# Buffers kept across stages, and a second pool for modulation weights, in a two-block transformer kernel

## The chip, the cores and the metric

The kernel runs on one core of one Trainium2 chip. The metric is the device time of one execution in microseconds (us). The core has five engines that run their own instruction queues and meet at semaphores: TensorE (PE; its weight loads are shown apart as PEld), VectorE (DVE), ScalarE (ACT), GpSimd (POOL) and SyncE (SP). In this kernel SP issues nearly all DMA transfers, in the order of its queue.

## What is computed

The input is one sequence of 512 tokens, 1024 wide, in float32. The reference, cut to the calls that matter:

```python
def first_block(x, c, ...):
    mod = (jax.nn.silu(c) @ w_ada + b_ada)            # six vectors of 1024
    sh1, sc1, gt1, sh2, sc2, gt2 = jnp.split(mod, 6, axis=-1)
    h = rmsnorm(x, norm1_g) * (1.0 + sc1) + sh1
    z = h @ w_in
    ...
    mix = concat([rmsnorm(nsa_attention(...)), rmsnorm(s5_mixer(...))])
    x = x + gt1 * (mix @ w_o)
    h = rmsnorm(x, norm2_g) * (1.0 + sc2) + sh2
    a, v = jnp.split(causal_dwconv(h @ w_up, conv_w, conv_b), 2, axis=-1)
    x = x + gt2 * ((jax.nn.silu(a) * v) @ w_down)
    return rmsnorm(x, normf_g)

def second_block(x, ...):
    x = x + short_conv_mixer(rms_norm(x, conv_norm), ...)
    x = x + dilated_attention_mixer(rms_norm(x, attn_norm), ...)
    return x
```

nsa_attention has three branches (compressed keys, selected blocks, a window) with a gate each; s5_mixer is a linear recurrence over 32 groups of channels; the dilated attention has three groups of 16 heads.

## The kernel before

The program goes through four stages, one after the other: the mixer of the first block (attention and S5, about 0 to 375 us), its feed-forward part (to 751), the convolution mixer (to 1194) and the dilated attention (to 1822). All of x stays in SBUF as four tiles of 128 tokens.

**Gemms.** Every float32 factor is split into a high and a low part, and a product is three matmuls: high by high, high by low, low by high. `wload` (L100) brings a piece of weights, at most 128x1024 float32 (512 KB), into a "raw" buffer; ACT makes the high part `whi` from it, DVE the low part `wlo`. The raw buffers, three of them, belong to the weight pool `W["p"]`. The activations are kept transposed, eight planes of 128 channels by 512 tokens, also as a high and a low part: `xh` and `xl` for the normalized x, `hh` and `hl` for what the inner part of a stage makes.

**Normalizing at a stage's border.** `scaled` (L300) turns the sums of squares of two token tiles into scales, with a dozen small DVE operations, and multiplies x by them into two "adaw" buffers (L323). `norm_t` (L341) has PE transpose those (L350); ACT then writes xh and DVE xl (L358, or L364 where a shift is added). The first half of the tokens is normalized ahead, inside the last projection of the stage before (the list `ahead`); the second half (`second`) comes when the first gemms of the new stage have done the first half's tokens. In the mixer, `ahead` gets its entry (L1241) just before the last part of the output projection, `out_a(1)`. `residual` (L391) adds a projection's result to x and takes the sums of squares on ACT.

**Modulation.** The vectors shift, scale and gate come from w_ada, in twelve halves of four pieces of 512 KB. `ada_rows` (L214) loads a piece (L221) into an "adaw" buffer and multiplies it on PE (L223); `ada` (L248) adds up and spreads. There are two "adaw" buffers in the pool b1p, and three things share them: these pieces, the weights of the key and value compression (`hidden`, L962, with its load at L978 and matmuls at L981), and the normalized x (L323). The mixer's parts are written down in the order of two strings; the letters e, f, h, i, j, l, m and n stand for a modulation half each, a digit for a block of 128 queries of the attention, G for the S5 gate, w and x for parts of the output projection:

```python
ORDER = "kvDBCAKc1lbVda0g"
ORDER2 = "032jGn1mehfwxi"
```

**S5.** `core_b` (L919) works on eight channel groups at a time. It loads a matrix `mi` in eight strips (L932), multiplies on PE (L954, L957) and sends its result out and in again by DMA (`yd`, `yt`).

**Order and storage.** The framework's scheduler, which has its own estimate of each operation's time, sets the order of every engine's instructions once, when the program is built. On the chip each engine goes through its list in order and waits where something isn't ready. Pools open and close with their stage. A tile whose storage was used by an earlier tile waits for the earlier one's last reader: in a pool's own ring, that of the tile's last use; where a new pool lies over the storage of a closed one, those of the tiles that lay there. Before, xh, xl, hh and hl are made anew in each stage, in that stage's pool; the second attention also makes `kbh` and `kbl` there, blocked keys, which are zeroed by four MEMSETs on GpSimd (L1299), and loads a small tile of gains, `qkg` (L1293), which DVE scales (L1294).

## Time and profile before

| | us |
|---|---|
| median of three runs (1816.0, 1817.91, 1825.29) | 1817.91 |
| profiled execution | 1823.86 |
| its span | 1822.1 |
| PE busy | 1751.0 (96%) |
| DVE busy | 1095.5 (60%) |
| ACT busy | 845.7 (46%) |
| GpSimd busy | 184.3 (10%) |
| mean granted TensorE clock | 0.991 |

The span is the time from the first instruction of the profile to its last; the profiled execution's own time has 1.76 us around it. Busy times overlap, since the engines run side by side. An idle time in a row stands in brackets, with the operation that ended it; the granted clock is a share of full speed. In a timeline, consecutive instructions of one kind stand in one row, with their number behind an x.

### The profile page before, as it was taken

How to read it: one execution, taken by the hardware profiler on the slowest of the kernel's cores; microseconds unless marked ns; L12 is line 12 of the kernel's file. 1: busy time of each engine (PE TensorE's matmuls, PEld its weight loads, DVE VectorE, ACT ScalarE, POOL GpSimd, SP SyncE). 2: the span in 40 equal slices, each digit the busy share in tenths (PEclk: the TensorE clock that was granted, in tenths of full speed). 3: DMA queues.
4: the chain of work that ended last, by engine and by line, in shares of the span. 5: the costliest groups of instructions: out<-in, count | busy, mean ns of one | idle time of the engine just before them, and what ended most of it. 6: DMA issues, size and time to landing. Idle time of an engine off the chain costs nothing.

```text
span 1822.1 us, 25899 instructions
## 1 busy us (share of the span) xinstructions
PE 1751.0 (96%) x9588; PEld 1441.2 (79%) x9588; DVE 1095.5 (60%) x2720; ACT 845.7 (46%) x1679; POOL 184.3 (10%) x179
## 2 busy tenths in 40 slices
PE   5899989999999999899999999999999999999999
PEld 3787746888888888788888888878888888888877
DVE  8895766865545557643333333644766766666676
ACT  3532656564423445532322323445655655656653
POOL 3764202001100110000000000000000000000000
PEclk9998999999999999999999999999999999999999
DMA  8357750332333335333333323533222322322221
GB/s 341 95 152 199 230 176 12 102 122 92 94 92 104 95 102 173 106 104 95 102 93 99 98 93 104 152 107 102 85 78 82 94 73 80 91 74 91 82 65 64
DMA packets 86782, 200.21 MB, mean 110 GB/s; under 512 B 32000, under 2 KB 36864, under 8 KB 86656
## 3 DMA queue, kind: packets, MB, share of 16 engines
q1 hardware_dynamic: 86656, 198.57, 35.3%
q8 instruction: 75, 1.23, 0.3%
q14 instruction: 51, 0.42, 0.1%
HBM read 193.75 MB, written 4.78 MB: 109 GB/s over the span
## 4 chain that ended last, share of the span: by engine, by line
PE 85%; DVE 7%; DMA 4%; ACT 2%; issue 1%; POOL 1%; SPq 0%; DVEq 0%; ACTq 0%; POOLq 0%
PE bank L128 38%; PE bank L141 35%; DMA adaw<-in_w_ada_dram 2%; DVE wlo L95 1%; PE bank L1163 1%; PE bank L1500 1%; PE bank L1470 1%; PE bank L1580 1%; PE bank L223 1%; PE bank L1159 1%; PE bank L1558 1%; PE bank L1140 1%; PE bank L1569 1%; PE bank L1587 1%; ACT whi L59 1%
## 5 line engine op out<-in xcount | busy, mean ns | idle before, releaser
L95 DVE TENSOR_TENSOR wlo<-raw,whi 128x1024 fp32r<-128x1024 f32 (+1 forms) x287 | 350.1, 1220 | 302.5 <-ACT whi L59 288.5
L59 ACT ACTIVATE whi<-raw 128x1024 fp32r<-128x1024 f32 (+1 forms) x287 | 299.4, 1043 | 473.7 <-PE bank L128 265.2
L128 PE MATMUL bank<-xh,whi 128*128 128x512 f32 (+1 forms) x1120 | 291.2, 379 | 10.7 <-ACT xh L59 10.6
L128 PE MATMUL bank<-xl,whi 128*128 128x512 f32 (+1 forms) x1120 | 288.3, 375 | 7.0 <-DVE xl L364 6.8
L128 PE MATMUL bank<-xh,wlo 128*128 128x512 f32 (+1 forms) x1120 | 283.6, 374 | 0.0
L128 PEld LDWEIGHTS bank<-xh,whi 128*128 128x128 f32 x1120 | 204.3, 191 | 52.8 <-ACT xh L59 13.8
L128 PEld LDWEIGHTS bank<-xl,whi 128*128 128x128 f32 x1120 | 203.9, 189 | 47.1 <-DVE xl L364 8.8
L128 PEld LDWEIGHTS bank<-xh,wlo 128*128 128x128 f32 x1120 | 202.4, 189 | 37.7
L141 PE MATMUL bank<-whi,xh 128*128 128x512 f32 (+2 forms) x800 | 209.2, 361 | 2.5 <-ACT v L59 1.2
L141 PE MATMUL bank<-wlo,xh 128*128 128x512 f32 (+2 forms) x800 | 205.1, 356 | 0.0
L141 PE MATMUL bank<-whi,xl 128*128 128x512 f32 (+2 forms) x800 | 204.9, 355 | 0.0
L141 PEld LDWEIGHTS bank<-wlo,xh 128*128 128x128 f32 x800 | 135.5, 190 | 22.5 <-issue 1.6
L141 PEld LDWEIGHTS bank<-whi,xl 128*128 128x128 f32 x800 | 135.2, 190 | 22.5 <-issue 1.6
L141 PEld LDWEIGHTS bank<-whi,xh 128*128 128x128 f32 x800 | 128.8, 189 | 21.2 <-issue 3.9
L141 PE MATMUL bank<-wlo,hh 128*128 128x512 f32 x304 | 95.0, 389 | 0.0
L141 PE MATMUL bank<-whi,hl 128*128 128x512 f32 x304 | 94.9, 389 | 0.0
L198 DVE SCALAR_TENSOR_TENSOR cy<-bank,taps,cy 128x384 f32<-128x384 f32 (+3 forms) x176 | 72.9, 477 | 32.5 <-ACT cy L59 32.5
L59 ACT ACTIVATE P<-P,stat 128x128 f32<-128x128 f32 (+1 forms) x192 | 79.8, 419 | 21.9 <-DVE stat L1478 15.7
L141 PE MATMUL bank<-whi,hh 128*128 128x512 f32 x304 | 89.8, 389 | 0.0
L534 POOL TENSOR_TENSOR cy<-cy,sz 128x512 f32<-128x512 f32 x16 | 28.8, 1801 | 436.5 <-ACT sz L59 436.5
L141 PEld LDWEIGHTS bank<-whi,hl 128*128 128x128 f32 x304 | 57.1, 188 | 11.9
L141 PEld LDWEIGHTS bank<-wlo,hh 128*128 128x128 f32 x304 | 57.0, 188 | 11.8
(384 smaller groups left out, 2322.3 us busy)
## 6 DMA issues: line engine op xcount, KB each, us to landing
raw<-in_conv_w_in_dram SPq DMA_DIRECT2D x64, 512.0 KB, 3.7
raw<-in_w_pair_dram SPq DMA_DIRECT2D x64, 512.0 KB, 3.8
adaw<-in_w_ada_dram SPq DMA_DIRECT2D x48, 512.0 KB, 5.1
raw<-in_w_up_dram SPq DMA_DIRECT2D x44, 512.0 KB, 3.7
raw<-in_w_down_dram SPq DMA_DIRECT2D x30, 512.0 KB, 3.5
raw<-in_conv_w_out_dram SPq DMA_DIRECT2D x24, 512.0 KB, 3.7
raw<-in_w_o_dram SPq DMA_DIRECT2D x12, 512.0 KB, 4.2
x<-in_x_dram SPq DMA_DIRECT2D x8, 512.0 KB, 5.2
```

Source lines behind the costliest of these rows:

```text
L59: return nc.scalar.activation(o, i, fn, **kw)
L95: (eng or V).tensor_tensor(lo, src, f(hi), op=OP.subtract)
L128: mm(ps[:, tok], a[:, q, j * 128:(j + 1) * 128], b[:, k0 + q, tok], start=n == 0 and i == 0 and h != 1, stop=n == len(w) - 1 and i == 3 * ...
L141: mm(ps, a[:, base + k0 + q, tok], b[:, q, :], start=first and n == 0 and i == 0 and o == 0, stop=last and n == len(w) - 1 and i == 3 * kn ...
L198: V.scalar_tensor_tensor(o, i, t, o, op0=OP.mult, op1=OP.add)
L223: mm(pb[32 * q:32 * q + 32, :256], csil[:, r * 4 + q, 3 - i:35 - i], raw[:, q * 256:(q + 1) * 256], start=i == i0 and r == 0, stop=i > i0 ...
L534: P.tensor_tensor(y, y, sz, op=OP.mult)
L1140: mm(ps[:, :n], qs[:, h, qt], kk[:, br, kvh, 0:n], start=kk is ksh, stop=kk is ksl)
L1159: transpose(pt[:, s * 128:(s + 1) * 128], prs[hl][:, j * 128:(j + 1) * 128], ident)
L1163: mm(po[par * 64:par * 64 + 64, kvh * 256:(kvh + 1) * 256], vsw[:, j, br, kvh * 64:kvh * 64 + 64], ptt[:, par, :], start=False, stop=br == ...
L1470: mm(ps[:, :nk * 256], a[:, natural(i)], b[:, j0:i + 1].rearrange("p j h k -> p (j h k)"), start=n == 0, stop=n == 2)
L1500: mm(ps[:, r * 256:(r + 1) * 256], a[:, natural(2 * rr + r)], b[:, 2 * rr + r].rearrange("p h k -> p (h k)"), start=n == 0, stop=n == 2)
```

## The change

It has four parts.

1. ORDER2 has the last modulation half, `i`, ahead of the output projection's parts `w` and `x`.
2. `ada_rows` takes a second pool: of the two pieces of a row, the first goes to an "adaw" buffer as before, the second to a "raw" buffer of the weight pool.
3. Two pools, `hp` and `nx`, are opened ahead of the feed-forward stage and stay open to the end. `nx` holds nxh and nxl, the normalized x of the three later stages. `hp` holds h0 and h1, two tiles of 128x8x512: the first eight planes of hh and hl in the feed-forward stage (three more planes each are made in the stage's own pool), hh and hl in the convolution, and in the second attention yh and the blocked keys. Those are now one tile, zeroed by one MEMSET.
4. At the end of the mixer, the first half's scaling gets the scheduler's high priority.

```diff
-ORDER2 = "032jGn1mehfwxi"
+ORDER2 = "032jGn1mehfiwx"
...
-        def ada_rows(n0, n1, i0, pool, bufs, at):
+        def ada_rows(n0, n1, i0, pool, bufs, at, more=None):
...
-                    raw = pool.tile([128, 1024], F32, name="adaw", bufs=bufs)
+                    raw = more.tile([128, 1024], F32, name="raw") if more and r else \
+                        pool.tile([128, 1024], F32, name="adaw", bufs=bufs)
...
-            for pb in ada_rows(which * 4 + 2 * half, which * 4 + 2 * half + 1, 2 * half, b1p, 2, acc):
+            for pb in ada_rows(which * 4 + 2 * half, which * 4 + 2 * half + 1, 2 * half, b1p, 2, acc, W["p"]):
...
+        hp = top.enter_context(tc.tile_pool(name="hp", bufs=1, reuse_waits="tile"))
+        nx = top.enter_context(tc.tile_pool(name="nx", bufs=1, reuse_waits="tile"))
+
+        def hidden():
+            return [hp.tile([128, 8, S], F32R, name=n) for n in ("h0", "h1")]
+
+        def normed():
+            return [nx.tile([128, 8, S], F32R, name=n) for n in ("nxh", "nxl")]
...
-            xh = ffp.tile([128, 8, S], F32R, name="xh")
-            xl = ffp.tile([128, 8, S], F32R, name="xl")
-            hh = ffp.tile([128, 11, S], F32R, name="hh")
-            hl = ffp.tile([128, 11, S], F32R, name="hl")
+            xh, xl = normed()
+            hh, hl = (Planes([h[:, k] for k in range(8)] + [ffp.tile([128, S], F32R, name=f"{n}{k}") for k in range(3)])
+                      for n, h in zip(("hh", "hl"), hidden()))
...
-            xh = cvp.tile([128, 8, S], F32R, name="xh")
-            xl = cvp.tile([128, 8, S], F32R, name="xl")
-            hh = cvp.tile([128, 8, S], F32R, name="hh")
-            hl = cvp.tile([128, 8, S], F32R, name="hl")
+            xh, xl = normed()
+            hh, hl = hidden()
...
-        E["ahead"].append((E["scaled"](0), False))
+        with tc.high_priority():
+            E["ahead"].append((E["scaled"](0), False))
         out_a(1)
...
-        yh = pp.tile([128, 8, S], F32R, name="yh")
+        yh, kb = E["hidden"]()
         yl = Planes([None] * 8)
-        xh = pp.tile([128, 8, S], F32R, name="xh")
-        xl = pp.tile([128, 8, S], F32R, name="xl")
+        xh, xl = E["normed"]()
...
-        kbh = [pp.tile([128, 4, 2, 128], F32R, name=f"kbh{i}") for i in range(2)]
-        kbl = [pp.tile([128, 4, 2, 128], F32R, name=f"kbl{i}") for i in range(2)]
-        for t in kbh + kbl:
-            P.memset(f(t), 0.0)
+        P.memset(f(kb), 0.0)
+        kbs = [kb[:, 2 * i:2 * i + 2].rearrange("p a (b h k) -> p (a b) h k", b=2, h=2) for i in range(4)]
+        kbh, kbl = kbs[0:2], kbs[2:4]
```

The diff doesn't show the order that the scheduler makes of this. Three places follow, before and after. A row has the line of its own kernel (the changed one's lines are up to ten higher), the operation, what it writes and reads with buffer numbers, and the size; an x at the end counts equal rows.

First pair: SP's queue in the S5 stretch, around 140 us. `adaw` and `raw` from in_w_ada_dram are modulation pieces, in_w_c1_dram the compression weights of the values, in_w_in_g_dram and in_w_glu_dram ordinary weights. Before:

```order
L221 DMA adaw_1748<-in_w_ada_dram 128x1024
L221 DMA adaw_1754<-in_w_ada_dram 128x1024
L109 DMA raw_3233<-in_w_glu_dram 128x1024
L932 DMA mi_1888<-kd_118 16x8x128 x7
L978 DMA adaw_1829<-in_w_c1_dram 128x1024
L932 DMA mi_1888<-kd_118 16x8x128
L927 DMA uu_1942<-ud_116 128x512
L978 DMA adaw_1835<-in_w_c1_dram 128x1024
L960 DMA yd_117<-wk_1809 128x512
L978 DMA adaw_1841<-in_w_c1_dram 128x1024
L978 DMA adaw_1847<-in_w_c1_dram 128x1024
L932 DMA mi_1944<-kd_118 16x8x128 x8
```

After:

```order
L109 DMA raw_2151<-in_w_in_g_dram 128x840
L968 DMA yd_117<-wk_1570 128x512
L986 DMA adaw_1829<-in_w_c1_dram 128x1024
L109 DMA raw_2157<-in_w_in_g_dram 128x840
L986 DMA adaw_1835<-in_w_c1_dram 128x1024
L109 DMA raw_2163<-in_w_in_g_dram 128x560
L222 DMA raw_3204<-in_w_ada_dram 128x1024
L940 DMA mi_1888<-kd_118 16x8x128 x8
L935 DMA uu_1942<-ud_116 128x512
L986 DMA adaw_1841<-in_w_c1_dram 128x1024
L986 DMA adaw_1847<-in_w_c1_dram 128x1024
L968 DMA yd_117<-wk_1809 128x512
```

The first two w_c1 loads have moved ahead of the `mi` loads, three w_in_g loads and one modulation piece have come between, and two modulation pieces of this place have moved further up.

Second pair: SP's queue at the end of the first attention's modulation loads, with the loads of w_o. Before:

```order
L221 DMA adaw_3719<-in_w_ada_dram 128x1024
L221 DMA adaw_4175<-in_w_ada_dram 128x1024
L221 DMA adaw_4181<-in_w_ada_dram 128x1024
L109 DMA raw_4097<-in_w_o_dram 128x1024
L109 DMA raw_4136<-in_w_o_dram 128x1024
L109 DMA raw_4241<-in_w_o_dram 128x1024
L109 DMA raw_4280<-in_w_o_dram 128x1024
```

After:

```order
L222 DMA raw_3733<-in_w_ada_dram 128x1024
L222 DMA adaw_3727<-in_w_ada_dram 128x1024
L222 DMA raw_3745<-in_w_ada_dram 128x1024
L222 DMA adaw_3739<-in_w_ada_dram 128x1024
L109 DMA raw_3782<-in_w_o_dram 128x1024
L109 DMA raw_3846<-in_w_o_dram 128x1024
```

Before, pieces of w_o stood between the modulation pieces higher up, and the last half (4175 and 4181, and two pieces further down) was split around the rest of w_o. Now the pieces alternate between the two kinds of buffer, up to the last (3739), and all of w_o comes behind them.

Third pair: ACT's list at the border of feed-forward and convolution. nsq is the square of a piece of x, whose sum it keeps; bank is a PSUM bank with transposes. Before:

```order
L59 ACTIVATE nsq_7232,xss_96<-x_2340 128x512
L59 ACTIVATE nsq_7237,xss_96<-x_2340 128x512
L59 ACTIVATE xh_7250<-bank_7256,cols_91 128x256
L59 ACTIVATE nsq_7240,xss_96<-x_2340 128x512
L59 ACTIVATE xh_7250<-bank_7265,cols_91 128x256
L59 ACTIVATE xh_7250<-bank_7274,cols_91 128x256
```

After:

```order
L59 ACTIVATE whi_7156<-raw_7154 128x1024
L59 ACTIVATE nsq_7121,xss_96<-x_2340 128x512
L59 ACTIVATE nxh_7262<-bank_7268,cols_91 128x256
L59 ACTIVATE nxh_7262<-bank_7277,cols_91 128x256
L59 ACTIVATE nxh_7262<-bank_7286,cols_91 128x256
L59 ACTIVATE nxh_7262<-bank_7295,cols_91 128x256
L59 ACTIVATE nsq_7124,xss_96<-x_2340 128x512
```

The writes of the normalized x have moved from behind the last squares (7229 to 7240, the last residual) to between those of the residual before it (7121 and 7124).

## Rows read from the trace of the kernel before

**Rows 1.** The page: span, and PE's busy time with its share.
```profile
span 1822.1 us, 25899 instructions
...
PE 1751.0 (96%) x9588; PEld 1441.2 (79%) x9588; DVE 1095.5 (60%) x2720; ACT 845.7 (46%) x1679; POOL 184.3 (10%) x179
```

**Rows 2.** PE's waits, whole span: wait, total us, times, longest.
```profile
PE bank L223 <- DMA adaw<-in_w_ada_dram: 19.7, 12, 11.6
```

**Rows 3.** Timeline of PE, S5 stretch: start, us, work, [idle before <-releaser].
```profile
152.94 1.97 PE L981 MATMUL bank<-adaw,wk 128*64 128x256 f32 x8 [2.99 <-DMA adaw<-in_w_c_dram]
...
173.55 1.95 PE L957 MATMUL bank<-xs,x 128*128 128x64 f32 x16
```

**Rows 4.** Timeline of SP's queue, S5 stretch (issue times of DMAs).
```profile
147.37 0.35 SPq L978 DMA_DIRECT2D adaw<-in_w_c_dram  x1
...
160.65 4.74 SPq L932 DMA_DIRECT2D mi<-kd  x8
```

**Rows 5.** By stretch: length, busy us (instructions) per engine, PEclk, DMA share, GB/s.
```profile
153.00:167.00 14.00, 14.00 (x63) 10.64 (x63) 2.24 (x4) 0.00 (x0) 1.50 (x2) 0.51 0.59 142
...
167.00:181.00 14.00, 14.00 (x118) 13.34 (x117) 7.49 (x13) 6.08 (x15) 4.47 (x4) 1.00 0.67 221
```

**Rows 6.** PE's waits from 200 to 300.
```profile
PE bank L223 <- DMA adaw<-in_w_ada_dram: 6.8, 8, 1.5
```

**Rows 7.** Timeline of PE, first attention.
```profile
247.44 0.64 PE L223 MATMUL bank<-adaw,csil 128*32 128x256 f32 x8 [1.46 <-DMA adaw<-in_w_ada_dram]
...
250.17 0.64 PE L223 MATMUL bank<-adaw,csil 128*32 128x256 f32 x8 [0.57 <-DMA adaw<-in_w_ada_dram]
```

**Rows 8.** By stretch: first attention, and the program's first 50 us.
```profile
212.00:252.00 40.00, 32.85 (x255) 18.64 (x250) 29.77 (x123) 23.68 (x70) 3.43 (x5) 1.00 0.60 198
...
0.00:50.00 50.00, 30.59 (x192) 17.98 (x196) 43.73 (x207) 20.79 (x41) 19.68 (x27) 1.00 0.81 311
```

**Rows 9.** DMA issues, 205 to 255, then 196 to 204: last, us to landing.
```profile
adaw<-in_w_ada_dram SPq DMA_DIRECT2D x16, 512.0 KB, 4.6
...
adaw<-in_w_ada_dram SPq DMA_DIRECT2D x2, 512.0 KB, 6.8
```

**Rows 10.** Timeline of PE, feed-forward to convolution.
```profile
744.81 0.39 PE L141 MATMUL bank<-whi,hl 128*128 128x512 f32 x1
...
751.47 1.22 PE L128 MATMUL bank<-xh,whi 128*128 128x256 f32 x4 [6.27 <-ACT xh L59]
```

**Rows 11.** Timeline of ACT, then DVE, at the same border.
```profile
750.96 0.46 ACT L59 ACTIVATE xh<-bank,cols 128x256 fp32r<-128x256 f32 x1
...
758.16 2.19 ACT L59 ACTIVATE x<-x,rs_ym 128x1024 f32<-128x1024 f32 x2 [2.95 <-DVE adaw L323]
...
764.35 3.17 ACT L59 ACTIVATE xh<-bank,cols 128x256 fp32r<-128x256 f32 x8 [4.00 <-PE bank L350]
...
757.37 1.42 DVE L323 TENSOR_SCALAR adaw<-x,rs_ym 128x1024 f32<-128x1024 f32 x2
...
764.86 3.32 DVE L358 SCALAR_TENSOR_TENSOR xl<-bank,cols,xh 128x256 fp32r<-128x256 f32 x8 [6.07 <-ACT xh L59]
```

**Rows 12.** By stretch, at the same border.
```profile
751.00:757.00 6.00, 4.05 (x17) 3.76 (x18) 5.32 (x23) 3.69 (x11) 0.00 (x0) 0.50 0.16 51
...
757.00:764.00 7.00, 7.00 (x60) 7.00 (x60) 1.72 (x4) 2.19 (x2) 0.00 (x0) 0.99 0.01 2
```

**Rows 13.** Timeline of PE, mixer to feed-forward.
```profile
375.48 3.28 PE L350 MATMUL bank<-ident,adaw 128*128 128x128 f32 x16 [3.80 <-DVE adaw L323]
```

**Rows 14.** Timelines of DVE, ACT, PE and GpSimd, convolution to second attention.
```profile
1198.86 0.17 DVE L1294 TENSOR_SCALAR qkg<-qkg 128x3 f32<-128x3 f32 x1 [1.96 <-DMA qkg<-in_qk_gain_dram]
...
1199.73 1.40 ACT L59 ACTIVATE xh<-bank,cols 128x256 fp32r<-128x256 f32 x3 [1.92 <-DVE xl L358]
...
1200.26 0.75 PE L128 MATMUL bank<-xh,whi 128*128 128x256 f32 x4 [2.15 <-ACT xh L59]
...
1194.32 1.85 POOL L1299 MEMSET kbh<- 128x1024 f32 x2 [40.93 <-PE bank L141]
```

## The prediction

> **What bounds the kernel now.** I began with the page's first part: TensorE (PE) is busy 1751.0 us of a span of 1822.1 us [rows 1]. That leaves 71.1 us in which PE stands still, and an edit that adds no arithmetic can only win from those, or from stretches in which PE runs at its lower clock. Next came the list of PE's waits: the largest entry is the wait for a piece of the modulation weights, 19.7 us in 12 places, 11.6 us of it one wait, the start of the program, which the change leaves alone [rows 2]. Then I took the places one by one, from the timelines and the tables by stretch, and compared the instruction order of both kernels there. The long gemm stretches of feed-forward, convolution and dilated attention keep PE full, and the change does not alter their work.
>
> The sums below are made against the profiled execution, 1823.86 us (1.76 us of it outside the span). It lies 5.95 us above the median of the three runs, 1817.91 us; I take the gain worked out on it off the median.
>
> **Part 1: more buffers for the modulation weights, first in the S5 stretch.** Before, each of the four 512 KB pieces of one modulation half goes through two "adaw" buffers, which the compression weights (L978) and the normalized x (L321) share. So on SP's queue the third and fourth piece, and then the first piece of the next compression weights, each stand behind a release by PE. That w_c transfer is issued at 147.37 [rows 4], and PE waits 2.99 us for it, to 152.94 [rows 3]. The granted clock then shows 0.51 from 153 to 167: 63 matmuls in 14.00 us, where the next 14.00 us at 1.00 hold 118 of much the same mixture [rows 5]. 63 of those would take 63/118 x 14 = 7.5 us, so the low level costs 6.5 us. Wait and clock together are 9.5 us.
>
> After, the second half-rows go to the weight pool's "raw" buffers, all four pieces are consumed at once, and SP issues both w_c pieces before the eight "mi" loads of the next group (first order pair). The w_c wait goes. What is late next is "mi". The eight loads of the last group can be issued only when PE has finished with the group before; issuing eight took 4.74 us [rows 4], and their landing I bound by the 4.6 to 6.8 us of the 512 KB pieces [rows 9] and take at 4.6, since they are small: 9.3 us from release to use. PE's work in between is 16 matmuls of L957 (1.95 us [rows 3]), two pieces of L981 (at full clock half of 1.97 us each [rows 3]), 26 matmuls of L141 and a few small ones, at the 0.119 us of 118 in 14.00 us [rows 5] 3.1 and 0.4 us: 7.4 us together. That is a new wait of about 1.9 us, and I allow 1.6 more for the loads of the group before, which now also stand behind a modulation piece that waits for a weight split on DVE. **Gain 6 us** (9.5 - 1.9 - 1.6). Ends: 9.5 if nothing takes the wait's place; 0 if a wait of 3 us comes back there and the clock falls with it.
>
> **Part 2: the same buffers in the first attention, and the half "i" moved forward.** From 200 to 300 PE waits 6.8 us in eight places for modulation pieces [rows 6]. From 212 to 252 it is busy 32.85 of 40 us [rows 8]. With two buffers a piece is asked for only when PE has done with the one two before it. The change has three more buffers in this stretch, and takes in 24 pieces where 15 stood before: 5 that came after 252, and the 4 of "i" that stood in the output projection near 360. One piece is 0.64 us of PE work [rows 7], a little less where the next matmul follows at once, so PE has 32.85 + 9 x 0.6 = 38.2 us to do, 1.6 us a piece. Does DMA keep up? The first 50 us of the program moved 311 GB/s [rows 8], at which 512 KB take 1.7 us. Four pieces can land ahead, the other 20 need 34 us, under the 38.2 us. **Gain 5.5 us** of the 6.8 (a wait here and there will stay, since SP issues in order). Ends: 6.8 if all waits go; 2 if the pieces come at 1.8 us each all through (43 us, against 38.2 + 6.8 before).
>
> There is a price: the loads of w_o now stand on SP behind all modulation pieces (second order pair). The last four pieces' worth of PE work, 6.4 us, and some 3 us of attention lie between the issue of the first w_o piece and its first matmul; a landing of 4.6 to 6.8 us [rows 9] and one split fit. I put it at nothing; without that cover it is a few us, once.
>
> The Trainium skill speaks against this part: "DMA: Bandwidth & Descriptors", section "Issuing engines are not separate DMA queues", has all transfers run on the same 16 engines, so that more of them in flight only share those. The trace agrees: the landing is 6.8 us where w_o and modulation pieces overlap, 4.6 us where they don't [rows 9]. By that rule the gain could come from asking earlier alone, and would be the lower end, 2, as soon as the shared engines slow the pieces down to 1.8 us.
>
> **Part 3: normalized x kept across stages, border of feed-forward and convolution.** This is the surest term. PE ends the down projection at 745.20 and stands until 751.47, for xh [rows 10], though the transposes that feed it were done inside that projection. ACT writes the first of them at 750.96 [rows 11], behind sums of squares of the last residual: the buffer is a new one, laid over storage that the stage before still holds. Then the low clock: 751 to 757 has it at 0.50, 17 matmuls in 4.05 us of busy time, where 757 to 764 at 0.99 does 60 in 7.00 [rows 12]. The second half's first xh is written at 764.35 [rows 11]. After, "nxh" is storage of its own, and ACT and DVE write the first half while the projection runs (third order pair). So PE goes on at 745.20 with the 72 matmuls of the first half, 72 x 7.00/60 = 8.4 us, to 753.6. What is late next is the second half: its statistics hang on the last residual, as before. DVE gave the normalized x at 757.37 [rows 11], with eight writes of xl in its way (3.32 us for eight [rows 11]), seven of them behind the last statistics; without those, about 754.5, two tiles of it to 755.9, then ACT scales x itself in 2.19 us [rows 11] ahead of the first xh: 758.1 against 764.35. **Gain 6.3 us**, with a new wait of 2 to 4 us between the two halves. Ends: 8 if ACT's scaling slips behind; 4 if PE falls to its lower clock in the new wait: 2 us, as much as the 17 matmuls lost in the row at 0.50 (4.05 against 17 x 0.117 = 2.0).
>
> The Trainium skill's "TensorE: Matmul & The Clock Gate", section "HAM oscillation — how this bites in real kernels", describes a loop in which each wait for a transfer leaves the clock low for the work behind it. By that rule the lower end, 4, would be the value. The trace has it both ways: low behind 152.94 and 751.47, full from 212 to 252 with its many waits [rows 8].
>
> **Part 4: border of convolution and second attention.** DVE waits 1.96 us for the small load of gains, "qkg", at 1198.86 and holds up the writes of xl; ACT's next xh waits 1.92 us for those, PE 2.15 us for that [rows 14]. The load is late because its storage was still in use. After, it is issued ahead of the last ten w_out loads, and its scaling leaves this spot. **Gain 2 us**; ends 1 (another step of that chain is late next) and 3 (the clock gains too). The zeroing of the key buffers changes from four MEMSETs, 1.85 us for two [rows 14], to one of four times the size, some 3.7 us on GpSimd, which has nothing else there; its first reader stands several gemms further on, so it costs nothing, and a few us if the last convolution matmul releases it late.
>
> **Part 5: priority at the border of mixer and feed-forward.** PE waits 3.80 us for the normalized x at 375.48 [rows 13]. In the new order DVE still has the whole last residual and the second half's sum ahead of it, in the same places. **Gain 0**, ends -0.5 and 0.8.
>
> **Sum:** 6 + 5.5 + 6.3 + 2 + 0 = 19.8 us. 1823.86 becomes 1804.1 for a profiled execution, 1817.91 becomes 1798 for the median. The upper ends give 9.5 + 6.8 + 8 + 3 + 0.8 = 28.1 (1790), the lower 0 + 2 + 4 + 1 - 0.5 = 6.5 (1811).
>
> **Rivals.**
> (a) *The waits only change their names.* In the S5 stretch the "mi" loads take the place of w_c and the clock falls as before, gain 0 to 1; in the attention the shared DMA engines leave 2 to 3. For it: SP issues in order, and each piece brings one more release to stand behind. Against it: the issue times of rows 4 leave room. 0.5 + 2.5 + 6.3 + 2 = 11: 1807, up to 1811.
> (b) *Slower: one queue, one pace.* If SP's waits chain the raw pieces to the adaw pieces, so that a piece still comes every 2.7 us as at 247.44 and 250.17 [rows 7], 24 pieces take 64.8 us against 38.2 us of PE work: 26.6 us of waits where 6.8 stood, 19.8 lost; by the same chain part 1 brings nothing, and 8.3 us remain from parts 3 and 4. 11.5 us slower: 1829. It decides from the pace at which 24p - 38.2 - 6.8 eats those 8.3 us, p = 2.2 us. Against it: two sets of buffers, released by different pieces.
> (c) *The priority does act*, and normalized x overtakes the last residual: 3.80 us more, 1794. Against it: the order.
> (d) *The pools do not do what they say*: the first half of xh still waits at 745, for a reader of the old contents. The gain at that border is then 0, the sum 13.5: 1804. Against it: the last reader of the feed-forward's xh is its up projection, long done.
>
> **How the numbers follow.** The forecast, with its own ends, 0.66; (a) 0.17; (b) 0.05; (c) 0.05; (d) 0.07. 0.5%, about what a measurement of this kernel can tell from no change, is 9.1 us: faster means under 1808.8. The forecast but for its low end (0.62), (c), (d) and over half of (a) (0.09) lie there: 0.83. Within 0.5%: the rest of the forecast and of (a): 0.12. Slower: (b), 0.05. The range takes in the forecast's ends with (a), (c) and (d), and a microsecond or two on either side: 1788 to 1812.
>
> **What would show it.** Right: no wait on w_c near 150 and a clock near 1 from 153 to 167; L223's waits from 200 to 300 under 2 us; PE on L128 at once after the down projection, then a wait of 2 to 4 us before the second half; ACT's xh near 1198 without its wait on DVE; 3.8 us still there near 370. Wrong: a wait on "mi" of 3 us with a low clock behind it, waits for pieces at a pace over 2 us, or PE standing at the first matmul with w_o.

## The result

The changed kernel takes 1800.75 us (median of six runs, 1797.64 to 1808.86); the kernel before, run beside it, 1821.48 us. The ratio is 0.9884, with a 95% interval of 0.9864 to 0.9904: about 21 us, or 1.2%, faster. In the profiled execution the span goes from 1822.1 to 1797.8 us, 24.3 us. The page of the changed kernel has PE busy for 13.7 us less than [rows 1], with the same 9588 matmuls:

```profile
span 1797.8 us, 25889 instructions
...
PE 1737.3 (97%) x9588; PEld 1436.8 (80%) x9588; DVE 1094.2 (61%) x2720; ACT 843.7 (47%) x1679; POOL 184.2 (10%) x176
```

So over half of the gain in this profile is the same work in less busy time, at the higher clock for longer and with matmuls that stand closer together; the rest is less standing still. PE's waits over the whole span, the largest of them (what is waited for; us in total, times, longest):

```profile
PE bank L224 <- DMA adaw<-in_w_ada_dram: 14.5, 4, 11.9
PE bank L351 <- DVE adaw L324: 8.4, 2, 6.1
...
PE bank L128 <- ACT nxh L59: 2.3, 4, 0.9
PE bank L989 <- POOL s L951: 2.1, 1, 2.1
```

The first line answers [rows 2]: 19.7 us in twelve places became 14.5 in four, 11.9 of it the start of the program. To see where the 24 us lie, I paired the matmuls of two traces by line, tiles and count, and took the difference of their starts (median over the 10 us from each mark on); minus is earlier than in the kernel before. The first four rows are this profile and a second one of the same kernel, and two of it without the moved half; the labels are those of the experiments below.

| profile, by us of before | 110 | 130 | 190, behind S5 | 310, behind attention | 400, in feed-forward | 800, in convolution | 1250, in 2nd attention |
|---|---|---|---|---|---|---|---|
| changed kernel | +0.6 | +4.2 | -5.2 | -13.3 | -14.7 | -21.1 | -24.0 |
| after_again | +1.3 | +5.1 | -0.9 | -7.7 | -8.9 | -14.9 | -17.8 |
| raw_pools | +0.9 | +3.6 | -2.3 | -11.5 | -7.2 | -13.3 | -16.2 |
| raw_pools_2 | 0.0 | +2.7 | -2.5 | -12.1 | -7.5 | -13.4 | -16.3 |
| raw_only | +0.5 | +2.2 | -7.3 | -18.5 | -14.6 | -14.7 | -14.6 |
| no_pools | +1.2 | +5.3 | -0.6 | -9.5 | -10.7 | -9.9 | -11.4 |
| pools_only | +0.2 | +1.1 | -6.1 | -2.3 | -3.2 | -9.6 | -12.5 |
| nx_only | +0.3 | +0.9 | -5.5 | -4.6 | -5.2 | -9.8 | -11.1 |
| no_raw | -0.2 | -0.1 | -6.4 | -4.2 | -4.4 | -10.6 | -13.5 |
| order_only | +0.3 | +1.9 | +0.5 | +7.1 | +7.0 | +7.6 | +8.1 |
| l_old | +0.3 | +1.3 | -6.1 | -17.5 | -17.5 | -23.9 | -26.8 |
| l_behind | +2.2 | +3.2 | -2.9 | -15.0 | -16.5 | -20.9 | -23.8 |
| gp_two | +1.5 | +5.2 | -0.6 | -9.4 | -9.0 | -13.6 | -16.5 |

**S5 stretch.** The table by stretch (length, busy us and instructions of each engine, clock, DMA share, GB/s) and PE's timeline, of the changed kernel:

```profile
143.00:150.00 7.00, 7.00 (x37) 7.00 (x37) 4.98 (x8) 2.28 (x4) 5.47 (x7) 0.53 0.96 328
153.00:167.00 14.00, 13.96 (x118) 11.81 (x117) 6.72 (x10) 3.41 (x9) 4.10 (x5) 1.00 0.78 229
...
212.00:252.00 40.00, 37.86 (x331) 23.45 (x330) 33.44 (x122) 25.93 (x70) 2.47 (x4) 1.00 0.85 290
```
```profile
121.44 1.08 PE L989 MATMUL bank<-adaw,wk 128*64 128x256 f32 x8 [2.13 <-POOL s L951]
```

Where [rows 5] had 63 matmuls at 0.51 there are 118 at 1.00. The low clock isn't gone, though: it comes 10 us sooner, with 37 matmuls from 143 to 150. And 3.6 us are lost ahead of it, between 110 and 130: a new wait at 121.44. The releaser named (s, on GpSimd) was long done; what PE had not got was the compression weight, issued on SP at 113.92. In the new order a 512 KB piece of w_in_a is loaded in front of it where the kernel before loaded 420 KB of w_in_g, and the two compression weights issued there land after 7.1 us (median) where they took 5.8. That the larger load is the whole cause is not shown: in pools_only, with the old order, they took 6.5.

**First attention.** The last row of that table answers [rows 8]: 331 matmuls where 255 stood, PE busy for 37.86 of 40 us. The pieces now come in pairs:

```profile
216.64 0.64 PE L224 MATMUL bank<-adaw,csil 128*32 128x256 f32 x8 [1.97 <-DMA adaw<-in_w_ada_dram]
...
220.08 0.64 PE L224 MATMUL bank<-adaw,csil 128*32 128x256 f32 x8
220.54 0.61 PE L224 MATMUL bank<-raw,csil 128*32 128x256 f32 x8
223.27 0.64 PE L224 MATMUL bank<-adaw,csil 128*32 128x256 f32 x8
```

A pair each 3.2 to 3.4 us is 1.6 to 1.7 us a piece, against 2.7 in [rows 7], and one wait of 1.97 us is left of the eight in [rows 6]. No wait for a piece of w_o has come in its place.

**Mixer to feed-forward.** PE's timeline, then VectorE's:

```profile
360.71 3.65 PE L351 MATMUL bank<-ident,adaw 128*128 128x128 f32 x16 [6.08 <-DVE adaw L324]
```
```profile
355.75 1.23 DVE L95 TENSOR_TENSOR wlo<-raw,whi 128x1024 fp32r<-128x1024 f32 x1 [0.97 <-ACT whi L59]
...
359.81 1.41 DVE L324 TENSOR_SCALAR adaw<-x,rs_yn 128x1024 f32<-128x1024 f32 x2
```

The wait of [rows 13] grew from 3.80 to 6.08 us. The moved half's matmuls no longer stand in the output projection, so PE comes to its end sooner (354.62), and VectorE's chain, with splits of the feed-forward's first weights in it, ends when it ends.

**Feed-forward to convolution.** PE's timeline:

```profile
730.12 0.39 PE L141 MATMUL bank<-whi,hl 128*128 128x512 f32 x1
730.34 0.64 PE L128 MATMUL bank<-nxh,whi 128*128 128x256 f32 x4
...
741.47 2.10 PE L351 MATMUL bank<-ident,adaw 128*128 128x128 f32 x16 [2.33 <-DVE adaw L324]
743.95 0.51 PE L128 MATMUL bank<-nxh,whi 128*128 128x256 f32 x2 [0.38 <-ACT nxh L59]
```

The 6.27 us of [rows 10] are gone, the first half runs straight on, and the wait before the second half is 2.33 us.

**Convolution to second attention.** ACT's and PE's timelines, in place of [rows 14]:

```profile
1177.39 1.40 ACT L59 ACTIVATE nxh<-bank,cols 128x256 fp32r<-128x256 f32 x3 [0.67 <-DVE nxl L359]
```
```profile
1177.92 0.74 PE L128 MATMUL bank<-nxh,whi 128*128 128x256 f32 x4 [0.91 <-ACT nxh L59]
```

VectorE's wait for the small load of gains is gone; PE waits 0.91 where it waited 2.15 us.

### The profile page after: what moved, and what is told of

Its sections match the earlier page's. It is cut to its first block, busy times and chain, and to the rows that moved or that the text cites. A ratio compares the mean times of both kernels' runs of the same rounds, so it can differ in the third digit from the quotient of the medians.

```text
span 1797.8 us, 25889 instructions
## 1 busy us (share of the span) xinstructions
PE 1737.3 (97%) x9588; PEld 1436.8 (80%) x9588; DVE 1094.2 (61%) x2720; ACT 843.7 (47%) x1679; POOL 184.2 (10%) x176
## 3 DMA queue, kind: packets, MB, share of 16 engines
q8 instruction: 75, 1.23, 0.3%
## 4 chain that ended last, share of the span: by engine, by line
PE 86%; DVE 8%; ACT 2%; DMA 2%; issue 1%; POOL 1%; SPq 0%; DVEq 0%; ACTq 0%; POOLq 0%
PE bank L128 38%; PE bank L141 36%; DVE wlo L95 1%; PE bank L1477 1%; PE bank L1171 1%; PE bank L1507 1%; PE bank L1148 1%; PE bank L1167 1%; PE bank L1587 1%; DMA adaw<-in_w_ada_dram 1%; PE bank L1565 1%; DVE h L1462 1%; PE bank L1576 1%; PE bank L1594 1%; PE bank L224 1%
## 5 line engine op out<-in xcount | busy, mean ns | idle before, releaser
L128 PE MATMUL bank<-nxh,whi 128*128 128x512 f32 (+1 forms) x1072 | 273.3, 375 | 2.3 <-ACT nxh L59 2.3
L128 PE MATMUL bank<-nxl,whi 128*128 128x512 f32 (+1 forms) x1072 | 271.7, 373 | 0.0
L128 PE MATMUL bank<-nxh,wlo 128*128 128x512 f32 (+1 forms) x1072 | 268.9, 373 | 0.0
L128 PEld LDWEIGHTS bank<-nxh,whi 128*128 128x128 f32 x1072 | 194.8, 189 | 39.3 <-ACT nxh L59 3.6
L128 PEld LDWEIGHTS bank<-nxl,whi 128*128 128x128 f32 x1072 | 194.4, 188 | 35.7
L128 PEld LDWEIGHTS bank<-nxh,wlo 128*128 128x128 f32 x1072 | 193.1, 188 | 35.6
L141 PE MATMUL bank<-whi,nxh 128*128 128x512 f32 x512 | 164.3, 401 | 1.2 <-ACT v L59 1.1
L141 PE MATMUL bank<-whi,h 128*128 128x512 f32 x576 | 160.3, 391 | 0.0
L141 PE MATMUL bank<-whi,nxl 128*128 128x512 f32 x512 | 158.7, 391 | 0.0
L141 PE MATMUL bank<-wlo,nxh 128*128 128x512 f32 x512 | 158.3, 390 | 0.0
L141 PEld LDWEIGHTS bank<-whi,nxl 128*128 128x128 f32 x512 | 96.0, 188 | 20.5
```

What stands on the lines that cost most here:

```text
L128: mm(ps[:, tok], a[:, q, j * 128:(j + 1) * 128], b[:, k0 + q, tok], start=n == 0 and i == 0 and h != 1, stop=n == len(w) - 1 and i == 3 * ...
L141: mm(ps, a[:, base + k0 + q, tok], b[:, q, :], start=first and n == 0 and i == 0 and o == 0, stop=last and n == len(w) - 1 and i == 3 * kn ...
```

## The experiments

My theory after the result: three separate gains, S5, attention and the two later borders, that add up. The rivals: one part carries it all; or the S5 gain isn't the change's. One part needed no run: in the built order of all engines and of SP's queue, the priority at the border changes no row, neither alone nor beside the other parts.

### One part alone: pools, buffers, order

pools_only keeps the two pools, raw_only the weight buffers (`more`), order_only the moved half:

```diff
-            for pb in ada_rows(..., 2 * half, b1p, 2, acc):
+            for pb in ada_rows(..., 2 * half, b1p, 2, acc, W["p"]):      # raw_only
-ORDER2 = "032jGn1mehfwxi"
+ORDER2 = "032jGn1mehfiwx"                                             # order_only
```

> Only the two kept pools (nxh, nxl, h0, h1 and the key buffers), nothing else of the change. My theory: the two later borders gain by themselves, 6.4 us between feed-forward and convolution (PE's 6.27 us wait for xh goes, a wait of 2 to 3 us before the second half's transposes comes) and 2.8 us between convolution and second attention (DVE's 1.96 us wait for qkg goes); the first 700 us keep their time. 9.2 us faster than before in the trace, about 1811 to 1813. Rival: the gain at the borders needs the earlier weight loads of the other parts, then under 5 us.

> Only the second pool for the modulation pieces. My theory: about 5 us in the S5 stretch (the 2.99 us wait for w_c and most of 13.7 us at the lower clock go), about 6 us of waits for pieces between 200 and 300, and the wait at the border of mixer and feed-forward stays at 3.8 us: 10 to 12 us faster than before, about 1809 to 1811. Rival: the S5 gain hangs on chance in the clock, then 5 to 6 us. Also open: whether the wait of 2.1 us and the low clock near 120 come with this part; I expect them here, since a 512 KB weight piece takes the place of a 420 KB one on the DMA engines there.

> Only the last modulation half moved ahead of the output projection. My theory: no gain, -2 to +3 us: with two buffers its four pieces wait in the attention at 2.7 us a piece, and in the output projection DVE's chain of residuals, not PE, sets the end, so the 2.4 us of PE work taken out there come back as a longer wait for the normalized x (6 us where 3.8 stood). Rival: PE work taken from a full stretch is a gain of 2.4 us there.

Measured, with the kernel before at 1822.65 beside them: pools_only 1812.79, ratio 0.9947 (0.9931 to 0.9964); raw_only 1816.22, 0.9968 (0.9941 to 0.9995); order_only 1825.28, 1.0014 (0.9993 to 1.0035). The pools bring what was expected, at the expected places: 6.4 and 2.9 us in their row of the table, between 400 and 800 and between 800 and 1250. The order alone brings nothing: its profile falls 6.6 us behind in the attention, 2.4 of it the work of the four moved pieces, and gets nothing back up to 400, since PE then waits longer for the normalized x (PE's timeline):

```profile
382.44 3.65 PE L351 MATMUL bank<-ident,adaw 128*128 128x128 f32 x16 [6.81 <-DVE adaw L324]
```

The rest of the 6.6 us is not the longer waits for pieces that I expected: those are 6.9 us in all, as before (6.8). It is the lower clock, in a place where no other profile has it that long (the same stretch of order_only, then of the kernel before):

```profile
219.00:233.00 14.00, 14.00 (x70) 8.31 (x67) 7.58 (x40) 4.82 (x18) 0.00 (x0) 0.51 0.38 124
```
```profile
219.00:233.00 14.00, 13.31 (x103) 7.52 (x103) 10.39 (x49) 8.93 (x28) 0.74 (x1) 1.00 0.59 186
```

The buffers bring 6.4 us by the medians, though the one profile was 14.7 us ahead: 11.2 us in the attention, 7.3 before it, and 3.9 given back at the mixer border.

### All but the order, and all but one other part

raw_pools undoes the moved half (and the priority), no_pools the pools, no_raw the buffers.

> The whole change but for the order of the last modulation half (the priority, which moves no instruction, is left out too). My theory: as fast as the changed kernel within 1.5 us, about 1800; the wait for the normalized x at the border of mixer and feed-forward is back from 6.1 to about 3.8 us. Rival: the moved half is worth 2.4 us or more, about 1803 to 1804.

> The changed kernel without the two pools of normalized x and inner activations (each stage has its own buffers again), with the moved half, the weight buffers and the border's priority kept. Theory: the pools are worth 6.4 us at the FFN-to-convolution border and 2.8 us at the convolution-to-attention border, whatever else is changed, so the time is 1800.8 + 9.2 = 1810, and the two borders read as in the kernel before (TensorE waits 6.3 and 2.2 us there). With the buffers alone at 1816.2 that also makes the moved half worth about 6 us beside the buffers. Rival: the moved half pays only where the pools are there too, then 1816 as with the buffers alone.

> The changed kernel with the second half of each modulation piece loaded into the two old buffers again; the moved half, the two pools and the border's priority kept. Theory: with two buffers the attention stage takes its pieces at one rate wherever they stand, so moving a fifth group into it only adds waits there (order alone: 8.4 us of piece waits, TensorE 6 us later by 240 us), and the time is that of the pools alone, 1812.8, plus 0 to 4 us: 1815. Rival: the moved half is worth by itself what it was worth beside the buffers (1808.8 - 1800.8 = 8 us), then 1805.

Measured: raw_pools 1808.78 us, 0.9927 (0.9911 to 0.9943), so 8 us short of the changed kernel where I had expected none; no_pools 1816.73, 0.9963 (0.9941 to 0.9986), as raw_only and not the 1810 of a plain sum, which is what its rival said; no_raw 1815.08, 0.9962 (0.9941 to 0.9983), as expected. With two buffers the attention waits as before, 7.2 us in nine places. The moved pieces, the last four, don't wait; they only add their work (no_raw, PE's waits from 200 to 300, then PE's timeline at one of those pieces):

```profile
PE bank L224 <- DMA adaw<-in_w_ada_dram: 7.2, 9, 1.4
```
```profile
274.73 0.64 PE L224 MATMUL bank<-adaw,csil 128*32 128x256 f32 x8
```

The surprise was raw_pools. Its S5 stretch stands in the same order as the changed kernel's, and yet (PE's timeline, then the table by stretch):

```profile
153.99 1.97 PE L962 MATMUL bank<-uu,mi 128*128 128x64 f32 x16 [1.84 <-DMA mi<-kd]
```
```profile
153.00:167.00 14.00, 13.01 (x68) 10.43 (x69) 3.50 (x7) 1.18 (x3) 1.69 (x2) 0.63 0.71 217
```

That is the wait for mi that the prediction allowed 1.9 us for, and behind it the lower clock, as before the change. So perhaps the 8 us were S5's and not the order's.

### The changed kernel and raw_pools, side by side

> The changed kernel itself, beside the same kernel without the moved half. Theory (the moved half pays): 1801 again, with most executions near 1800. Rival (the 8 us between 1800.8 and 1808.8 lie in the state space stage, whose instructions stand in the same order in both: in the three other profiles with the weight buffers and TensorE's wait of 1.8 us for mi near 153 us the half clock lasts 10 us from 155 on, in that of the changed kernel it had none there): then some executions fall near 1808 here too, and the profile of one of those shows the wait for mi and the half clock near 155.

> The changed kernel without the moved half and without the border's priority, a second time, beside the changed kernel. Theory (the moved half pays 8 us): 1808.8 again, all executions above 1806. Rival (the state space stage's half clock comes in some executions and not in others): some executions near 1801 to 1803, and a difference to the changed kernel of 2 to 4 us only.

Measured: after_again 1803.27 us (1798.89 to 1805.78), 0.9884 (0.9867 to 0.9902); raw_pools_2 1807.91 (1807.27 to 1810.52), 0.9917 (0.9903 to 0.9931). This time the changed kernel's profile, span 1804.0 us, shows the wait and the clock as well, and the full clock where the first profile had the low one:

```profile
155.36 2.72 PE L962 MATMUL bank<-uu,mi 128*128 128x64 f32 x16 [1.72 <-DMA mi<-kd]
```
```profile
143.00:150.00 7.00, 6.63 (x59) 6.63 (x60) 6.29 (x11) 2.67 (x5) 6.78 (x8) 1.00 0.96 321
...
153.00:167.00 14.00, 12.29 (x62) 9.50 (x61) 5.00 (x8) 1.01 (x2) 3.18 (x4) 0.63 0.68 194
```

The rival holds for S5: the same instructions, 118 matmuls at 1.00 in one execution and 62 at 0.63 in the other, 4.3 us apart by 190 in the first table. In the first profile PE, slowed from 143 to 150, came to the matmuls that need mi at 155.78, 10.8 us after SP began to issue its loads, and didn't wait; in the second it came at 153.64, 7.8 us after, and waited. So the first outcome is not one without the low clock, but one with less of it, and none behind a wait for mi.

But the moved half does pay beside the buffers. Between 190 and 400 the two profiles of the changed kernel gain 9.5 and 8.0 us, the two of raw_pools 4.9 and 5.0: in the attention they are 1 to 3 us behind, since the moved pieces are work there, and from 310 to 400 they gain 1.2 to 1.4 where raw_pools loses 4.3 to 4.6 (there PE waits 5.00 and 4.43 us for the normalized x, 3.80 in the kernel before, and new are 1.1 to 1.3 us for a weight split and 1.0 us for nxh). That is 3 to 4.6 us, and the medians side by side are 4.6 us apart; the 8 us between runs at different times were more than that. Without the pools the medians show none of it (no_pools 1816.73, raw_only 1816.22), but their intervals leave room for it, so the rival of no_pools is neither shown nor excluded.

### The buffers, but not in S5

l_old leaves the one half that lies in the S5 stretch, "l", in the two old buffers.

```diff
-        def ada(which):
+        def ada(which, spread=True):
...
-            ... b1p, 2, acc, W["p"]):
+            ... b1p, 2, acc, W["p"] if spread else None):
...
-    halves = {"efhijlmn"[i]: (lambda i=i: ada(2 + i // 2)) for i in range(8)}
+    halves = {"efhijlmn"[i]: (lambda i=i: ada(2 + i // 2, i != 5)) for i in range(8)}
```

> The changed kernel with the one modulation piece group that lies in the state space stage (l) loaded into the two old buffers, and all groups after it half into the weight buffers. Theory: the weight buffers cost TensorE 3.6 us near 121 us and bring 8.9 us later in that stage, and it is the attention stage where they pay for certain (8 us, and 2.4 behind); with l in the old buffers the stage reads as before the change (no wait near 121 us, 1 to 3 us for w_c near 150 us, half clock behind it or not), so the time is that of the changed kernel plus 3 us, between 1798 and 1806, with executions near 1808 gone if these come from the wait for mi. Rival: the weight buffers' gain is mostly the state space stage's, then 1808 or more.

Measured, beside after_again: 1801.54 us (1796.79 to 1802.02), 0.9871 (0.9855 to 0.9888), so 1.7 us under the changed kernel, less than the two intervals can tell apart, and not the rival's 1808. By the times, the S5 stretch doesn't need the buffers. PE still waits for the compression weight, but keeps its clock in this profile, that of the fastest of the four runs (timeline, table by stretch):

```profile
152.23 1.08 PE L989 MATMUL bank<-adaw,wk 128*64 128x256 f32 x8 [1.83 <-DMA adaw<-in_w_c_dram]
```
```profile
153.00:167.00 14.00, 13.12 (x108) 10.82 (x104) 3.70 (x6) 1.29 (x2) 1.50 (x2) 1.00 0.79 215
```

Five profiles have an S5 stretch in the old order (before, order_only, pools_only, nx_only, no_raw), and l_old and l_behind have it but for two loads, where pieces of a later half stand in place of w_glu. Of these seven, before and order_only are at 0.51 and 0.55 from 153 to 167, the other five at 1.00. Of the seven with the buffers there, five wait 1.7 to 2.4 us for mi or uu and are at 0.63 to 0.67 (after_again, both of raw_pools, no_pools, gp_two). The first of the changed kernel and raw_only are at 1.00 there, with no such wait, and at 0.53 ten us sooner (37 and 36 matmuls in 7 us). So with the buffers every profile loses the clock somewhere in S5.

### Which pool does what

nx_only adds to the kernel before the pool of normalized x alone:

```diff
+        nx = top.enter_context(tc.tile_pool(name="nx", bufs=1, reuse_waits="tile"))
+        def normed():
+            return [nx.tile([128, 8, S], F32R, name=n) for n in ("nxh", "nxl")]
-            xh = ffp.tile([128, 8, S], F32R, name="xh")
-            xl = ffp.tile([128, 8, S], F32R, name="xl")
+            xh, xl = normed()
...
```

> The kernel before with the pool of normalized x alone (two tiles kept over FFN, convolution and gated attention). Theory: it is the normalized x that the next stage's first products wait for at the FFN-to-convolution border, since the FFN's buffers there are released only after its last product; so this pool has all of the 6.4 us there and the pool of inner activations has only the 2.8 us at the next border: 1822 - 6.4 = 1816. Rival: the gain at the first border comes from the inner activations' place, then 1822 here; or both borders need only this pool, then 1813 as with both.

Measured: 1816.52 us, 0.9963 (0.9941 to 0.9984), the 1816 of the theory. PE goes straight from the down projection to the convolution:

```profile
739.59 0.39 PE L141 MATMUL bank<-whi,hl 128*128 128x512 f32 x1
739.82 0.64 PE L128 MATMUL bank<-nxh,whi 128*128 128x256 f32 x4
```

Its profile gains 4.6 us there, with PE at the lower clock behind the border, and 1.3 us at the next; pools_only, at the full clock, 6.4 and 2.9. So the pool of x carries the first border; part of the second belongs to the other pool, of which no run shows what it does alone.

### The mixer border: the low halves on GpSimd

```diff
-            wa, wb = wload(w0, 8, 256), wload(w1, 8, 256)
+            wa, wb = wload(w0, 8, 256, eng=P), wload(w1, 8, 256, eng=P)
```

> The changed kernel with the low halves of the first two weights of the FFN and of the convolution split on GpSimd instead of VectorE (4 splits of 1.2 us at each border). Theory: at the mixer-to-FFN border VectorE's chain sets the end (two of these splits stand ahead of the last residual there, TensorE waits 6.1 us), so the wait falls by about 2.2 us there, and by up to 1 us at the FFN-to-convolution border (wait 2.3 us): 1800.8 - 3 = 1798. Rival: GpSimd's splits take longer and end after the first products want them, or the longer wait only brings TensorE's half clock, then 1800 to 1804.

Measured: 1808.56 us (1807.54 to 1814.83), 0.9924 (0.9897 to 0.9951): not faster. The wait before the first half's transposes grew instead, as GpSimd's, VectorE's and PE's timelines show:

```profile
353.95 5.26 POOL L95 TENSOR_TENSOR wlo<-raw,whi 128x1024 fp32r<-128x1024 f32 x2 [27.96 <-DVE rs_mn L175]
362.91 2.40 POOL L95 TENSOR_TENSOR wlo<-raw,whi 128x1024 fp32r<-128x1024 f32 x1 [3.69 <-ACT whi L59]
```
```profile
354.48 2.38 DVE L165 TENSOR_SCALAR rs_yn<-rs_mn 128x2 int32<-128x2 int32 x1
356.89 2.34 DVE L168 TENSOR_TENSOR rs_un<-rs_yn 128x2 f32<-128x2 f32 x1
...
363.02 2.30 DVE L170 SCALAR_TENSOR_TENSOR rs_yn<-rs_un,rs_yn 128x2 f32<-128x2 f32 x1
```
```profile
366.26 3.37 PE L351 MATMUL bank<-ident,adaw 128*128 128x128 f32 x16 [7.72 <-DVE adaw L324]
```

Three operations of 128x2 of the chain, which take 0.15 to 0.17 us elsewhere, took 2.38, 2.34 and 2.30, each until one of GpSimd's splits was done. The Trainium skill has this ("SBUF — State Buffer", section "Who interferes with whom"): a VectorE instruction with two inputs in SBUF excludes a GpSimd one that reads SBUF, one in a two-port mode excludes any GpSimd one that needs the shared ports, and whoever is second stands until the first is done. The trace agrees, with 6.5 us added to a chain from which the change took three splits of 1.23 us; in which mode the first of the three ran, a TENSOR_SCALAR with one input, it doesn't show. At the next border two of VectorE's operations on x took 2.46 and 2.02 us beside GpSimd's splits, and PE's wait there is 3.56 us instead of 2.33. By the first table gp_two trails the changed kernel's first profile by 7.5 us at 1250: 2.9 of them come between 190 and 800, and 4.6 are S5's, where gp_two has the wait for mi and the low clock.

### The mixer border: the same splits behind the chain

l_behind is l_old with these splits held, on VectorE, behind the first half's two normalized tiles:

```diff
-            wa, wb = wload(w0, 8, 256), wload(w1, 8, 256)
+            with tc.issue_after(last[0].ins) if behind else ExitStack():
+                wa, wb = wload(w0, 8, 256), wload(w1, 8, 256)
```

> The kernel with l in the old buffers, and with VectorE's three low-half splits of the FFN's first weights (1.23 us each) put behind the first half's two normalized tiles at the mixer-to-FFN border. Theory: VectorE's chain sets that border (from 348.9 to 361.2 us in the trace of the changed kernel: reduce, eleven small operations of the reciprocal root with splits and residuals between them, then the two tiles), so taking 3.7 us out of it lets TensorE go on 2 to 3.7 us sooner (a wait of 3 to 4.5 us for adaw where it is now 6.1 to 6.8): 1801.5 - 3 = 1798.5. Rivals: the splits then stand ahead of the low halves of x (nxl) and TensorE waits there for the same time, so 1801.5; or the shorter wait also keeps TensorE's clock up over the border (half clock for 6.8 us there now), then up to 3.4 us more, 1795.

VectorE's timeline, then PE's of l_old and of l_behind:

```profile
355.86 1.42 DVE L327 TENSOR_SCALAR adaw<-x,rs_yn 128x1024 f32<-128x1024 f32 x2
357.19 1.22 DVE L95 TENSOR_TENSOR wlo<-raw,whi 128x1024 fp32r<-128x1024 f32 x1
```
```profile
357.76 3.65 PE L351 MATMUL bank<-ident,adaw 128*128 128x128 f32 x16 [6.81 <-DVE adaw L324]
```
```profile
356.76 2.10 PE L354 MATMUL bank<-ident,adaw 128*128 128x128 f32 x16 [3.24 <-DVE adaw L327]
360.21 2.17 PE L128 MATMUL bank<-nxh,whi 128*128 128x256 f32 x16 [1.34 <-ACT nxh L59]
...
372.19 1.30 PE L128 MATMUL bank<-nxh,whi 128*128 128x256 f32 x7 [1.34 <-ACT nxh L59]
```

The chain was what PE waited for: the wait is 3.24 us instead of 6.81, and the 16 transposes behind it take 2.10 us at full clock where they took 3.65. But two waits of 1.34 us for ACT's nxh are new, and from 310 to 400 the profile gains 1.5 us on l_old's. The time, 1800.82 us (1799.74 to 1803.58), 0.9881 (0.9865 to 0.9898), is l_old's and the changed kernel's. Most of a shortened wait came back as the next ones, and at the next border this profile lost 2 us to the lower clock (below, part 3).

## Why the prediction was right, and where it was not

**The total** was near: 1798 forecast, 1800.75 measured, 1803.27 when measured again. Side by side with the kernel before (1821.48, then 1823.77) that is 20.7 and 20.5 us where 19.8 were forecast; the median of three that the forecast started from was 4 to 6 us low. In the profiled executions, against 1823.86 us, 24.3 and 18.1 us came. That the total is so near is in part luck: parts 3 and 4 were right in place and size, part 2 was too small, and part 1, too large, made up for it.

**Part 1, S5: 6 us forecast, 5.2 in the first profile, 0.9 in the second.** The step that failed is the wait for mi that was booked without the clock. Its size was right (1.9 us; 1.7 to 1.9 for mi, and 2.4 for uu in one profile), but the sum took back all 6.5 us of low clock, and with the buffers the clock fell again in all seven profiles: in five behind that wait, in two some 10 us ahead of it. The end given as "0 if a wait of 3 us comes back there and the clock falls with it" is what those five show, at a shorter wait. Rival (a) had this half of the story. The loss near 121 (some 2 to 4 us) I had not seen.

The other doubtful step is that the 9.5 us of wait and low clock in the one trace of before were taken as the kernel's: five of the seven profiles with the old or nearly the old order have the full clock from 153 to 167. Which outcome is the usual one stays open. The profile of before lies 5.95 us above the median of its three runs, but next to the medians of the later runs (1821.48 to 1823.77), so it is no odd one; and the five at full clock lie 1.1 to 5.0 us below their kernels' medians. At 190 the profiles with the buffers stand 0.6 to 7.3 us ahead of that of before, the other six from 0.5 behind to 6.4 ahead. By the medians raw_only gains 6.4 us, less than the 7.3 that its profile gains between 190 and 400 alone, and l_old, without the buffers in S5, is no slower. So a gain of the buffers in S5 is not shown.

**Part 2, attention and the moved half: 5.5 forecast, 9.5 and 8.0 measured between 190 and 400.** The mechanism was right: 1.6 to 1.7 us a piece (1.7 estimated), PE busy 37.86 us between 212 and 252 (38.2 worked out). The sum was too small because it counted PE's waits alone; the prediction's first paragraph had let a gain come only from waits and from the lower clock. The tables by stretch of the kernel before and of the changed one, over the same 1437 matmuls but one:

```profile
190.00:400.00 210.00, 192.77 (x1436) 146.56 (x1435) 151.93 (x501) 125.98 (x311) 21.92 (x25) 0.98 0.38 123
```
```profile
184.80:385.30 200.50, 186.34 (x1437) 146.70 (x1436) 151.56 (x501) 124.64 (x311) 21.34 (x25) 0.98 0.39 126
```

PE stands still for 17.2 us in the first and 14.2 in the second, 3.1 less: the waits for pieces fell by 5.4 (7.4 to 2.0), and the mixer border gave 2.3 of that back. The other 6.4 us are busy time, at the same mean clock. Half of it lies in the matmuls of the pieces, the same 224 in both (the same stretches, these matmuls alone):

```profile
190.00:400.00 210.00, 19.52 (x224) 5.30 (x224) 0.98 0.38 123
```
```profile
184.80:385.30 200.50, 16.22 (x224) 6.07 (x224) 0.98 0.39 126
```

That is 3.3 us, and I put it to the pairs: the eight matmuls of a piece alone are 0.64 us, where another piece follows at once it starts 0.45 us later (220.08 and 220.54 above), and 24 pieces now stand in pairs. Another part is where the low clock lies: in the kernel before some of it falls into full work near 290 and costs 1.7 us by estimate, 0.34 of this row's 5 us, while in the changed kernel all of it is at the mixer border, in part in the wait of 6.08 us:

```profile
289.00:294.00 5.00, 5.00 (x29) 3.80 (x28) 3.60 (x12) 1.83 (x7) 0.09 (x1) 0.66 0.00 0
```

The rest I have not traced.

The rule of the Trainium skill on the shared DMA engines ("DMA: Bandwidth & Descriptors", section "Issuing engines are not separate DMA queues") would have had 2, by the prediction's reading. The pieces did share them (290 GB/s against 198 in [rows 8]), but not down to 1.8 us a piece, and rival (b)'s 2.7 did not come.

**Part 3: 6.3 forecast, 6.4 measured** (5.9 to 6.4 in seven profiles with both pools), with a wait of 2.33 us where 2 to 4 were allowed. The lower end, 4, which the Trainium skill's loop of waits and low clock ("TensorE: Matmul & The Clock Gate", section "HAM oscillation — how this bites in real kernels") would have made the value, is seen twice, each time with the lower clock behind the border: nx_only, 4.6 us, and l_behind, 4.4 (gp_two's 4.6 has the longer wait). In l_behind PE waits the same 2.33 us as in the changed kernel, and the clock falls in the one and not in the other (l_behind, then the changed kernel):

```profile
741.00:748.00 7.00, 6.34 (x31) 5.83 (x29) 3.23 (x8) 3.79 (x10) 0.00 (x0) 0.51 0.00 0
```
```profile
743.00:750.00 7.00, 6.03 (x47) 5.39 (x46) 4.39 (x9) 4.55 (x10) 0.00 (x0) 1.00 0.00 0
```

Rival (d) is out.

**Part 4: 2 forecast, 2.9 measured.** The zeroing took 3.52 us on GpSimd (3.7 expected), and held up one small VectorE operation until it ended; PE did not see it:

```profile
1173.23 3.52 POOL L1304 MEMSET h<- 128x4096 f32 x1 [40.93 <-DMA raw<-in_w_pair_dram]
```
```profile
1175.86 0.92 DVE L175 TENSOR_SCALAR rs_mn<-nss 128x2 f32<-128x2 f32 x1
```

**Part 5: 0 forecast, and 0 by the built order;** rival (c) is out. But its premise, "3.8 us still there", was wrong: 6.08, because part 2 takes the moved pieces from in front of that wait (order_only, with the moved half alone, has 6.81; pools_only, without it, 3.83). The prediction put their work into the attention and did not ask what they had covered.

What stays open is how often each outcome of S5 comes, and with it whether l_old beats the changed kernel: fourteen profiles are too few to count by. Nor is S5 the only place with more than one outcome: no_pools took 1809.30 to 1821.22 us in ten runs, with a profile at 1812.35 that has S5's low clock already, and order_only's profile has another low stretch in the attention.

## What to carry to other kernels

A stretch at the lower clock behind a short wait is an outcome of one execution, not yet a property of the kernel: before it is booked as a gain, look for it in a second profile, and ask whether the new waits won't bring it back. Where the profiled time lies to a median of three runs doesn't tell: here it was the three that lay low. A piece of work that is moved away from a border was cover for whatever ends there; ask what that chain's own end is. And storage that the next stage writes should not lie over storage that the last one still reads: that was the surest part, and the first half's wait was gone in every combination.

## What the runs showed of the hardware

The same instruction order gave 118 matmuls in 14 us at a granted clock of 1.00 and 62 at 0.63, after a wait of 1.72 us in the second case; a wait of 1.83 us near the same place, in l_old, left the clock at 1.00. At the border of feed-forward and convolution a wait of 2.33 us left it at 1.00 in the changed kernel and was followed by 0.51 in l_behind. GpSimd's operations on 128x1024 (5.26 us for two, 2.40 for one) held VectorE's smallest ones (0.15 to 0.17 us) until they ended, in gp_two, and take about twice as long as VectorE's own split (1.23 us). Even its zeroing of 128x4096, which reads nothing, held one up, a TENSOR_SCALAR of 128x2 that took 0.91 or 0.92 us in each of the nine profiles with the two pools.
